# Two mixers that project convolution, keys, values and queries first and the recurrence last

## The chip, the cores and the metric

The kernel runs on one NeuronCore of a Trainium2 chip. TensorE (PE) does matmuls and transposes, VectorE (DVE) and ScalarE (ACT) the elementwise work, GpSimd (POOL) a little of it, SyncE (SP) issues nearly all loads. Each engine takes its own list of instructions strictly in order and meets the others through semaphores. The metric is the device time of one execution in microseconds.

## The reference, cut to what matters

Two conformer-like layers are followed by a state-space and mixture-of-experts block. Each of the two layers is a feed-forward part, a *mixer*, and a second feed-forward part, with a layer norm behind each. The change lies in the mixer alone:

```python
def _mixer(x, w_in, ...):
    u = x @ w_in                       # 512 tokens x 1792 columns
    u_conv, u_lru, q, k, v = jnp.split(u, [o1, o2, o3, o4], axis=-1)
    y_conv = _conv_module(u_conv, ...)  # gate, 31 taps, layernorm, silu
    y_lru = _recurrent(u_lru, ...)      # 4 taps, two gates, linear scan, * gelu
    y_attn = _swa(q, k, v, ...)         # window of 128, blocks of 128, sinks
    return jnp.concatenate([y_conv, y_lru, y_attn], axis=-1) @ w_out
```

Attention works on four blocks of 128 queries, each with 256 keys (block 0 with 128): scores, bias and mask, softmax with a sink, and the product with the values.

## The kernel before, in words

Every fp32 product of the projections is made of three fp32r matmuls (`mm3`, L114 to L116): high half by high half, high by low, low by high. So each 512 KB weight unit that is loaded into one of four `raw` buffers is split by ACT (L81, high half) and DVE (L82, low half) into `whl`. `Stream` holds the units of the whole kernel in one fixed order; a raw buffer is loaded anew as soon as it is free. In the mixers that order is: 14 units of `w_in`, 16 units of `ada_w` (the second block's modulation), 8 units of `w_out`.

The mixer's input, transposed, lies in `xTh` and `xTl`. Fourteen projections `pj(i)` read it, each 24 matmuls into one PSUM bank: 0 to 3 convolution, 4 and 5 the recurrence's input, 6 and 7 its gelu gate, 8 keys, 9 values, 10 to 13 queries. The first half of 0 to 3 is made in the stage before. What a projection leaves in its bank is taken away by a helper: `post_conv`, `post_xb` (one ACT instruction, then three DVE taps L384, giving `xc`), `post_gb` (gelu), `post_k`, `post_v`, `post_q` (`qh` by ACT L407, `ql` by DVE L408). The 31 taps of each convolution half are 62 DVE instructions (L372, L374, accumulator `acc`), put in as background work: `drain(n)` takes n of them.

`lru_gates` multiplies `xc` by gate matrices (bank `gt`, four fp32 matmuls) and takes a sigmoid; `lru_scan` does exp, tanh, square and square root on ACT, two products on POOL and a scan on DVE. `scores(b)` makes four banks `sc` on PE; DVE adds the bias and takes the maximum (L470), ACT does eight exps (L477), then DVE and ACT scale four probability tiles each (L486, L484). `pv(b)` is a generator: PE transposes the probabilities (`tp`), ACT and DVE copy them (`pT`), PE multiplies by the values (`yv`), and ACT and DVE write the result into rows 2 to 5 of `xTh` and `xTl`, over the mixer's input. `mod(n)` runs n of eight modulation steps, each four fp32 matmuls that read two raw buffers of `ada_w` (L855). `conv_ln` normalises the convolution by transposing it (`cn`, `cb`). `down` then multiplies `xTh` and `xTl` by `w_out` (`dn`, L222).

The text of the program gives priorities; a scheduler at build time sets the order on each engine from them and from its own estimate of durations. There are two mixers with the same code, stage 1 (its first 512-wide projection starts at 406.07 us) and stage 4 (1332.1 us). Each has a *first stretch* (the 512-wide projections) and a *second* (from the last projection to the first `dn`).

## Time and profile before

| | |
|---|---|
| median of 3 runs | 2941.47 us (2941.44 to 2942.12) |
| profiled execution | 2941.92 us, of which the span is 2940.1 us |
| PE busy | 2871.8 us, 98% |
| DVE busy | 1343.4 us, 46% |
| ACT busy | 1001.8 us, 34% |
| POOL busy | 188.1 us, 6% |
| HBM traffic | 158 GB/s over the span |

PE is busy nearly all the time, so a change matters by the microseconds in which PE waits, or runs at the lower clock, in the stage that is changed. The profile's line numbers are those of the kernel before; in the kernel after, everything behind the new constant stands two lines lower, and what follows the new lines of `pv` eight lower.

### The profile page before, as it was taken

What the parts mean: (1) busy time and instruction counts of PE and PEld (TensorE: products, weight loads), DVE (VectorE), ACT (ScalarE), POOL (GpSimd) and SP (SyncE); (2) the same over time, 40 slices, a digit from 0 to 9 for tenths busy, and PEclk for the clock granted to TensorE, in tenths of its full rate; (3) what the DMA queues carried; (4) which work ended last, traced back from release to release, by engine and by line L of the source; (5) the groups of instructions that cost most, each with busy time, mean ns of one, the idle gap of its engine ahead of it and who ended that gap; (6) DMA issues with size and microseconds to landing.
All of it is one profiled execution on the core that took longest, in us unless ns stands there. A gap on an engine that the chain in (4) does not pass through costs nothing.

```text
span 2940.1 us, 35337 instructions
## 1 busy us (share of the span) xinstructions
PE 2871.8 (98%) x14404; PEld 2199.5 (75%) x14404; DVE 1343.4 (46%) x2163; ACT 1001.8 (34%) x1589; POOL 188.1 (6%) x167
## 2 busy tenths in 40 slices
PE   8999998999999999999999999999999999999998
PEld 7888885888888878887588888878778886454453
DVE  4223398533335333359653234778874343222222
ACT  4222355422324122344552223567642321110011
POOL 0000001000000000001000000123330020000000
PEclk9999999999999999999999999999999999999999
DMA  6432334333323263232533323232243356899997
GB/s 196 114 99 79 94 111 153 98 104 115 93 79 98 96 205 115 78 104 79 180 118 108 98 79 105 80 108 79 87 137 130 95 206 263 341 407 427 427 427 325
DMA packets 104260, 465.93 MB, mean 158 GB/s; under 512 B 12838, under 2 KB 13494, under 8 KB 79521
## 3 DMA queue, kind: packets, MB, share of 16 engines
q1 hardware_dynamic: 95936, 435.81, 41.5%
q0 software_dynamic: 6720, 23.13, 2.7%
q10 hardware_dynamic: 1440, 4.72, 0.4%
q8 instruction: 113, 1.85, 0.2%
q14 instruction: 51, 0.41, 0.0%
HBM read 457.73 MB, written 5.88 MB: 158 GB/s over the span
## 4 chain that ended last, share of the span: by engine, by line
PE 81%; DVE 9%; DMA 6%; ACT 2%; POOL 1%; issue 1%; SPq 0%; DVEq 0%; POOLq 0%; ACTq 0%
PE dn L222 19%; PE pg L114 6%; PE pg L115 6%; PE pg L116 6%; PE pu L115 5%; PE pu L114 5%; PE pu L116 5%; DMA er<-in_eu 3%; PE ey L1673 3%; PE eu L1673 2%; PE eg L1673 2%; PE pj L115 2%; PE pj L114 2%; PE pj L116 2%; PE ga L1673 2%; DVE acc L374 2%
## 5 line engine op out<-in xcount | busy, mean ns | idle before, releaser
L82 DVE TENSOR_TENSOR whl<-raw,whl 128x1024 fp32r<-128x1024 f32 (+1 forms) x385 | 486.8, 1268 | 694.6 <-ACT whl L81 694.1
L81 ACT ACTIVATE whl<-raw 128x1024 fp32r<-128x1024 f32 (+1 forms) x385 | 405.7, 1056 | 652.3 <-PE pu L116 249.8
L222 PE MATMUL dn<-whl,hhl 128*128 128x512 f32 x2112 | 492.9, 395 | 0.0
L222 PEld LDWEIGHTS dn<-whl,hhl 128*128 128x128 f32 x2112 | 397.4, 188 | 92.4
L114 PE MATMUL pg<-xTh,whl 128*128 128x512 f32 x768 | 300.3, 391 | 0.0
L116 PE MATMUL pg<-xTh,whl 128*128 128x512 f32 x768 | 298.9, 389 | 0.0
L115 PE MATMUL pg<-xTl,whl 128*128 128x512 f32 x768 | 298.9, 389 | 0.0
L114 PE MATMUL pu<-xTh,whl 128*128 128x512 f32 x704 | 274.6, 390 | 0.0
L116 PE MATMUL pu<-xTh,whl 128*128 128x512 f32 x704 | 274.0, 389 | 0.0
L115 PE MATMUL pu<-xTl,whl 128*128 128x512 f32 x704 | 273.9, 389 | 0.0
L114 PE MATMUL pj<-xTh,whl 128*128 128x256 f32 (+1 forms) x688 | 231.4, 336 | 0.0
L115 PE MATMUL pj<-xTl,whl 128*128 128x256 f32 (+1 forms) x688 | 224.6, 326 | 0.0
L116 PE MATMUL pj<-xTh,whl 128*128 128x256 f32 (+1 forms) x688 | 224.6, 326 | 0.0
L114 PEld LDWEIGHTS pg<-xTh,whl 128*128 128x128 f32 x768 | 144.2, 188 | 36.9 <-issue 7.4
L116 PEld LDWEIGHTS pg<-xTh,whl 128*128 128x128 f32 x768 | 144.1, 188 | 30.2
L115 PEld LDWEIGHTS pg<-xTl,whl 128*128 128x128 f32 x768 | 144.3, 188 | 29.2
L292 ACT ACTIVATE sg<-pg 128x512 f32<-128x512 f32 x80 | 47.9, 598 | 320.8 <-PE pg L116 320.8
L116 PEld LDWEIGHTS pu<-xTh,whl 128*128 128x128 f32 x704 | 132.2, 188 | 27.6
L114 PEld LDWEIGHTS pu<-xTh,whl 128*128 128x128 f32 x704 | 132.1, 188 | 27.6 <-ACT x L1292 0.2
L115 PEld LDWEIGHTS pu<-xTl,whl 128*128 128x128 f32 x704 | 132.1, 188 | 27.4 <-issue 0.2
L295 DVE SCALAR_TENSOR_TENSOR h<-sg,pu 128x512 f32<-128x512 f32 x74 | 50.9, 688 | 198.9 <-PE pu L116 198.9
L115 PEld LDWEIGHTS pj<-xTl,whl 128*128 128x128 f32 x688 | 131.4, 191 | 10.9 <-issue 0.5
(485 smaller groups left out, 3996.4 us busy)
## 6 DMA issues: line engine op xcount, KB each, us to landing
raw<-in_wgu SPq DMA_DIRECT2D x176, 512.0 KB, 3.5
er<-in_eu SPq DMA_DIRECT2D x64, 1024.0 KB, 19.0
er<-in_eg SPq DMA_DIRECT2D x64, 1024.0 KB, 18.0
er<-in_ed SPq DMA_DIRECT2D x56, 1024.0 KB, 19.2
raw<-in_wd SPq DMA_DIRECT2D x88, 512.0 KB, 3.5
raw<-in_win SPq DMA_DIRECT2D x76, 512.0 KB, 3.5
raw<-in_ada_w SPq DMA_DIRECT2D x48, 512.0 KB, 4.5
raw<-in_wout SPq DMA_DIRECT2D x16, 512.0 KB, 5.0
```

The lines of the kernel that those rows point to most:

```text
L81: k.nc.scalar.activation(hi, r, AF.Copy)
L82: k.nc.vector.tensor_tensor(out=lo, in0=r, in1=hi.bitcast(F32), op=OP.subtract)
L114: mm(out, l[0], r[0], start=start, stop=False)
L115: mm(out, l[0], r[1], start=False, stop=False)
L116: mm(out, l[1], r[0], start=False, stop=stop)
L222: nc.tensor.matmul(banks[t, dh], l[:, s], r[:, dh * 512:(dh + 1) * 512], start=(u == 0 and n_l == 0), stop=(u == last and n_l == 2))
L292: nc.scalar.activation(sg, pg, AF.Silu)
L295: return nc.vector.scalar_tensor_tensor(h, sg, 0.5, pu, op0=OP.mult, op1=OP.mult)
L374: nc.vector.scalar_tensor_tensor(acc[:, j:], y[:, :T - j], wj, acc[:, j:], op0=OP.mult, op1=OP.add)
L1673: return tc.keep_in_program_order(nc.tensor.matmul(*args, **kw))
```

## The change

The order of the mixer's work is rewritten. After the convolution's projections come keys, values and the four queries; then the scores of block 0, projection 4, the scores of block 1, projection 5, the four gate products, block 0's product with the values, projection 6, the scores of block 2, projection 7, block 1's product with the values between the two scans, and the scores of block 3. The weight units are loaded in the same order (`MIXER`). Since projections 6 and 7 still read `xTh`, block 0's result can't be written there yet: ACT copies it from PSUM into a spare tile `yv` first, and the two writes follow later. The modulation steps stand behind projection 7, behind block 1 and behind the scores of block 3; those that are left follow in `mod(16)` as before.

```diff
@@ -27,6 +27,8 @@
 AHEAD = 2
 RAWS = 4
 SPLITS = 7
+
+MIXER = (0, 1, 2, 3, 8, 9, 10, 11, 12, 13, 4, 5, 6, 7)
 MODS = {1: {13: 1}, 3: {f: 1 for f in range(6, 14)}, 4: {13: 1}}
 PER = 1
 ROWS = {1: (0,), 3: (1,), 4: (2,)}
@@ -353,7 +355,7 @@
             w.ensure(u + 4)
             self.proj(u, bank[i], cols)
             w.done(u)
-            self.mod(MODS[st].get(i, 0))
+            self.mod(MODS[st].get(MIXER.index(i), 0))
 
         conv = []
 
@@ -508,6 +510,12 @@
                     nc.tensor.matmul(y[g * 64:g * 64 + 64], vn[0][:, vb * 128 + g * 64:vb * 128 + g * 64 + 64], pt[g],
                                      start=(kb == kbs[0]), stop=(kb == 1))
                 yield
+            if b == 0:
+
+                t = self.unit(name="yv")
+                nc.scalar.activation(t, y, AF.Copy)
+                y = t
+                yield
             bs = slice(b * 128, b * 128 + 128)
             yv = y.rearrange("p (r q) -> p r q", r=4)
             nc.scalar.activation(self.xTh[:, 2:6, bs], yv, AF.Copy)
@@ -553,54 +561,48 @@
                 post_conv(i // 2)
                 self.bg += [lambda c=i // 2, j=j: tap(c, j) for j in range(TAPS)]
             self.drain((0, 0, 4, 4)[i])
-        for c in range(2):
-            pj(4 + c)
-            post_xb(c)
-            self.drain(3)
-        for c in range(2):
-            pj(6 + c)
-            self.drain(7)
         self.load_band()
-        for c in range(2):
-            lru_gates(c)
-        for c in range(2):
-            post_gb(c)
         pj(8)
         post_k()
-        lru_scan(0)
-        self.drain(6)
+        self.drain(5)
         pj(9)
         post_v()
-        lru_scan(1)
-        self.drain(6)
+        self.drain(5)
         for r in range(4):
             pj(10 + r)
             post_q(r)
-            self.drain(6)
+            self.drain(5)
             if r == 0:
                 v_nat()
+        run = lambda *gs: [0 for g in gs for _ in g]
+        scores(0)
+        pj(4)
+        post_xb(0)
+        self.drain(3)
+        scores(1)
+        pj(5)
+        post_xb(1)
+        for c in range(2):
+            lru_gates(c)
+        p0 = pv(0)
+        for _ in range(3):
+            next(p0)
+        pj(6)
+        self.drain(3)
+        scores(2)
+        pj(7)
+        run(p0)
+        for c in range(2):
+            post_gb(c)
+        lru_scan(0)
+        run(pv(1))
+        self.mod(PER)
+        lru_scan(1)
+        self.drain(5)
+        scores(3)
+        self.mod(PER)
         for c in range(2):
             self.split_to(c, lru[c])
-        per = PER
-        run = lambda *gs: [0 for g in gs for _ in g]
-        scores(0)
-        self.drain(5)
-        self.mod(per)
-        scores(1)
-        self.drain(5)
-        self.mod(per)
-        p0 = pv(0)
-        next(p0)
-        self.mod(per)
-        run(p0)
-        scores(2)
-        self.drain(5)
-        self.mod(per)
-        p1 = pv(1)
-        next(p1)
-        self.mod(per)
-        run(p1)
-        scores(3)
         self.drain(1000)
         cl = conv_ln()
         run(zip(range(3), cl))
@@ -1956,9 +1958,11 @@
                     else:
                         steps, back = a["wgu"][l, j // 2], a["wd"][l, j // 2]
                     todo = self.mods(st)
-                    self.u_in[st] = []
+                    self.u_in[st] = [None] * 14 if j == 1 else []
                     for i in range(14 if j == 1 else NF):
-                        for m in range(steps[i].shape[0]):
+                        if j == 1:
+                            self.u_in[st][MIXER[i]] = w.add(steps[MIXER[i]][0])
+                        for m in range(0 if j == 1 else steps[i].shape[0]):
                             self.u_in[st].append(w.add(steps[i][m]))
                         n = MODS.get(st, {}).get(i, 0)
                         self.add_mod(todo[:n])
```

On PE, before, the first rows show the gate products (`gt`) among the projections, and the end of the last projection with a modulation step and the first scores (`sc`) behind it.

```order
L116 MATMUL pj<-xTh,whl 128x512
L423 MATMUL gt<-xc,lruw 128x512 x4
L114 MATMUL pj<-xTh,whl 128x512
...
L116 MATMUL pj<-xTh,whl 128x512
L855 MATMUL mod<-raw,cs 32x512 x4
L463 MATMUL sc<-kh,qh 128x128 x2
```

On PE, after, the first piece stands between projections 5 and 6, the second behind projection 7.

```order
L118 MATMUL pj<-xTh,whl 128x512
L425 MATMUL gt<-xc,lruw 128x512 x4
L500 MATMUL tp<-ident,S 128x128 x8
L510 MATMUL yv<-pT,vn 64x512 x2
L116 MATMUL pj<-xTh,whl 128x512
...
L118 MATMUL pj<-xTh,whl 128x512
L857 MATMUL mod<-raw,cs 32x512 x4
L500 MATMUL tp<-ident,S 128x128 x8
L857 MATMUL mod<-raw,cs 32x512 x17
L510 MATMUL yv<-pT,vn 64x512 x2
```

The gates, block 0's transposes and its product now stand in front of projection 6, and 21 of the 32 modulation matmuls stand around block 1's transposes, behind all projections.

On DVE, before, the taps of the recurrence (`xc`) alternate with the convolution's (`acc`) while PE does projections.

```order
L374 SCALAR_TENSOR_TENSOR acc<-yin,pc,acc 128x505
L384 SCALAR_TENSOR_TENSOR xc<-pj,pc,xc 128x511
L374 SCALAR_TENSOR_TENSOR acc<-yin,pc,acc 128x504
L384 SCALAR_TENSOR_TENSOR xc<-pj,pc,xc 128x510
L374 SCALAR_TENSOR_TENSOR acc<-yin,pc,acc 128x503
```

On DVE, after, the first `xc` stands among the work of the softmax of blocks 0 and 1 (`ISA` is the bias and maximum of L470, `sm` the softmax's small columns).

```order
L376 SCALAR_TENSOR_TENSOR acc<-yin,pc,acc 128x492
L481 TENSOR_TENSOR sm<-sm 128x8
L472 ISA S,sm<-sc,bias,sinks 128x256
L472 ISA sm 128x1
L482 RECIPROCAL sm<-sm 128x8
L386 SCALAR_TENSOR_TENSOR xc<-pj,pc,xc 128x511
L488 TENSOR_SCALAR S<-S,sm 128x128 x4
L386 SCALAR_TENSOR_TENSOR xc<-pj,pc,xc 128x510
L472 ISA S,sm<-sc,bias,sinks 128x256
L472 ISA sm 128x1
L386 SCALAR_TENSOR_TENSOR xc<-pj,pc,xc 128x509
```

The recurrence's taps moved behind all of block 0's and part of block 1's bias and maximum, and behind convolution taps that stood elsewhere before.

On ACT, after, the piece from block 0's `pT` to the exp of the first scan reads as follows.

```order
L505 ACTIVATE pT<-tp 128x512
L516 ACTIVATE yv<-yv 128x512
L417 ACT_TABLE_LOAD
L417 ACTIVATE gl<-pj 128x512
L479 ACT_TABLE_LOAD
L479 ACTIVATE S,sm<-S,sm 128x256 x8
L480 ACTIVATE sm<-sm 128x8
L521 ACTIVATE xTh<-yv 128x4x128
L486 ACTIVATE S<-S,sm 128x256 x4
L417 ACT_TABLE_LOAD
L417 ACTIVATE gl<-pj 128x512
L435 ACT_TABLE_LOAD
```

Before, one table load served both gelus and stood ahead of all exps of the softmax; now gelu and exp alternate, and the copy to the spare tile stands in between.

## Rows read from the trace of the kernel before

**Rows 1.** Windows: us, busy us (x) of PE, PEld, DVE, ACT, POOL; clock; DMA; GB/s.

```profile
406.07:464.54 58.47, 58.47 (x255) 46.79 (x253) 54.92 (x70) 24.78 (x32) 9.33 (x6) 1.00 0.20 66
464.54:508.08 43.54, 33.66 (x224) 16.53 (x223) 32.56 (x121) 28.27 (x88) 1.87 (x3) 0.86 0.67 231
...
1390.60:1435.07 44.47, 34.01 (x227) 16.58 (x226) 32.77 (x122) 29.49 (x93) 2.57 (x4) 0.88 0.68 228
```

**Rows 2.** Waits of PE, 390 to 560 us: us in total, times, longest.

```profile
PE sc L463 <- DVE ql L408: 3.4, 1, 3.4
PE yv L508 <- ACT pT L503: 3.0, 1, 3.0
...
PE tp L498 <- DVE S L486: 1.6, 1, 1.6
```

**Rows 3.** Waits of PE, 1320 to 1500 us.

```profile
PE yv L508 <- ACT pT L503: 2.5, 2, 2.2
...
PE dn L222 <- DVE ab L864: 1.9, 1, 1.9
```

**Rows 4.** Timeline of PE: start, duration in us, then the instruction; idle before.

```profile
427.86 3.59 PE L423 MATMUL gt<-xc,lruw 128*128 128x512 f32 x8
...
486.53 0.39 PE L463 MATMUL sc<-kh,qh 64*128 64x256 f32 x2
...
488.16 1.09 PE L498 MATMUL tp<-ident,S 128*128 128x128 f32 x8
489.18 3.26 PE L855 MATMUL mod<-raw,cs 128*32 128x512 f32 x14
492.37 1.07 PE L508 MATMUL yv<-pT,vn 128*64 128x512 f32 x2
...
503.71 1.97 PE L508 MATMUL yv<-pT,vn 128*64 128x512 f32 x2 [3.00 <-ACT pT L503]
...
508.08 1.20 PE L222 MATMUL dn<-whl,xTh 128*128 128x512 f32 x2
```

**Rows 5.** Timeline of DVE, same columns.

```profile
412.55 0.75 DVE L384 SCALAR_TENSOR_TENSOR xc<-pj,pc,xc 128x511 f32<-128x511 f32 x1
413.22 0.73 DVE L374 SCALAR_TENSOR_TENSOR acc<-yin,pc,acc 128x504 f32<-128x504 f32 x1
413.87 0.74 DVE L384 SCALAR_TENSOR_TENSOR xc<-pj,pc,xc 128x510 f32<-128x510 f32 x1
...
459.46 4.57 DVE L374 SCALAR_TENSOR_TENSOR acc<-yin,pc,acc 128x497 f32<-128x497 f32 x6
463.94 0.68 DVE L408 SCALAR_TENSOR_TENSOR ql<-pj,qh 128x512 fp32r<-128x512 f32 x1
...
474.71 0.35 DVE L470 CUSTOM_DVE_ANT_0 S<-sc,bias,sinks 128x128 f32<-128x128 f32 x1
...
474.98 0.34 DVE L470 CUSTOM_DVE_ANT_0 S<-sc,bias,sinks 128x128 f32<-128x128 f32 x1
...
477.28 0.48 DVE L470 CUSTOM_DVE_ANT_0 S<-sc,bias,sinks 128x256 f32<-128x256 f32 x1
...
477.68 0.48 DVE L470 CUSTOM_DVE_ANT_0 S<-sc,bias,sinks 128x256 f32<-128x256 f32 x1
```

**Rows 6.** Timeline of ACT, same columns.

```profile
432.20 1.28 ACT L415 ACT_TABLE_LOAD   x1
433.49 1.09 ACT L415 ACTIVATE gl<-pj 128x512 f32<-128x512 f32 x2
...
485.52 1.71 ACT L484 ACTIVATE S<-S,sm 128x256 f32<-128x256 f32 x4
...
492.19 0.51 ACT L477 ACTIVATE S<-S,sm 128x256 f32<-128x256 f32 x1 [2.67 <-DVE sm L473]
...
496.13 0.19 ACT L478 ACTIVATE sm<-sm 128x8 f32<-128x8 f32 x1
```

**Rows 7.** Line 63 (loads to raw buffers), 463 to 500 us.

```profile
DMA to landing us min/median/max: 3.6/4.7/8.1
```

## The prediction

> **What bounds the kernel now.** I read the shares of busy time first (PE 98%), then windows over the first mixer's two stretches, then PE's waits there, then the timelines of PE, DVE and ACT, and last the time that a load takes to land. The windows show where time can be won. In the first stretch, 58.47 us, PE is busy throughout at full clock, with DVE busy 54.92 of it. In the second, 43.54 us, PE is busy 33.66 and the granted clock is 0.86; the second mixer's is alike, 44.47 and 34.01 [rows 1]. PE waits there for `ql`, for `pT` and for scaled probabilities [rows 2], in the second mixer for `pT` and, at the first `dn`, 1.9 us for DVE's `ab` [rows 3]. After its 3.0 us wait a `yv` product takes 1.97 us where one at full clock takes 1.07 [rows 4]: PE is at its lower level of 1.2 GHz until about the first `dn`.
>
> What PE would need there at full clock: 32 modulation matmuls at 0.456 (14 records, two to a matmul, in 3.19 us), 14.6; 40 transposes at 0.125, 5.0; 7 `yv` at 0.5, 3.5; 48 score pairs, 5.7 (a block of 256 keys takes 1.5, from 486.53 to 488.16); 8 `cn`, 1.1 [rows 4]. That is 29.9, so 13.6 of 43.54 us are waiting and low clock. Both mixers lose some 27 us: more than that can't be won.
>
> **The change, step by step (first mixer).** Up to 406.07 nothing moves. A projection takes 5.46: the first stretch less 3.5 for the gates [rows 4] and 0.4 for a transpose, over 10 [rows 1].
>
> *Queries.* Six projections and the transpose end at 439.2. The last `ql` follows six convolution taps on DVE; at 0.65 each where two accumulators alternate (the `acc` between two `xc`) [rows 5] it ends at 441.3, and PE waits 1.1 at the end of block 0's scores, against 3.4 [rows 2].
>
> *The recurrence's gates.* Projection 4 ends at 447.0, block 1's scores at 448.5, projection 5 at 453.9. Then PE wants `xc`. DVE's list from that `ql` to the last tap of the second `xc`: 8 bias-and-maximum at 0.27 and 8 at 0.40, 5.4; 6 `xc` taps at 0.65, 3.9; 15 convolution taps, of which 8 follow their own accumulator at 0.75 (six in 4.48 us) and 7 alternate at 0.65, 10.6; scaling and small columns 1.5 [rows 5]. Sum 21.4: the second `xc` is there at 462.7, the first at 455.5. PE waits 1.6, does two gates (1.7), waits 5.5 and does two more.
>
> *Block 0.* ACT can start block 1's exps only at 458.8, behind DVE; eight take 3.94, the table for the sigmoid 1.28, a gate 0.6, four scalings 1.65, three gates 1.8, `pT` 0.6 [rows 6]: 468.7, and DVE's `pT` about 469.5. PE's transposes were done at 465.5, so it waits 4.0. It resumes at 470.5 with projection 6, after 12.2 us of waiting since 439. None of the modulation steps, which fill PE's waits before, stands here.
>
> *The clock.* PE did little from 454 to 470, so projection 6 will begin at 1.2 GHz, as the `yv` at 503.71 does. No row shows a projection after such a wait; bounds are 0 and 5.5, the whole of it at half speed. The nearest row, that `yv`, lost 0.9; I take 1.2. Projection 7 then ends at 484.2. PE has 23.7 us left to the first `dn` (29.9 less four of the scores, transposes and products done): 507.9 without any wait, where before has 508.08 [rows 4]. So the gain is gone by here, and each later wait is a loss.
>
> *Modulation.* With four raw buffers two of eight steps are loaded; 17 matmuls then stand in one piece and reach into the sixth step. A pair of buffers is freed, loaded and used again in 0.9 plus a landing. Landings there took 3.6 to 8.1 us, median 4.7 [rows 7]; I take 4.5. Steps 1 and 2 are done at 489, steps 3 to 5 at 492, 494.7, 497.5, the sixth's first matmul at 498.7; block 1's product, block 3's scores, `cn`, the last steps, block 2's transposes follow, with a wait for step 8's buffers. The first `dn` is due about 513.4, 5.5 us of waits later than without any.
>
> *The first units of `w_out`.* Their buffers come free only with step 7, at about 507; before, they were asked for at 491. The first split ends at 513, just in time. Behind it on ACT stand the exp table (1.28) and block 3's eight exps (3.94) and only then the second split (1.05): 519.3 [rows 6]. PE has 9 `dn` and a product to do, 2.6 us, and waits about 3.3.
>
> *Costed at nothing:* the copy to the spare tile (0.6 on ACT, in a stretch where ACT waits for projection 6), and the recurrence's last POOL and DVE work, which ends before the first `dn`. Block 3's probabilities are ready near 521, `dn`'s list reaches them near 526; if that cover fell away it would cost up to 2.
>
> *Sum:* 513.4 − 508.08 + 3.3 = 8.6, say 9 in the first mixer; in the second 7, since the 1.9 at `dn` is hidden there. 16 us on the profiled execution's 2941.9 (span 2940.1 and 1.8 around it; 0.5 above the median of the runs): **2958**.
>
> A page speaks against the change more strongly: the Trainium skill, ScalarE: Activation LUTs, "What ACT_TABLE_LOAD costs", counts a drain of some 1.4 us on top of each load's 1.28. The trace shows the load at 432.20 and the gelu that needs it at 433.49 [rows 6], so 1.28 is all of it here. By the page the five loads between block 0's copy and block 1's `pT` would delay that `pT` by 6.9 more, past PE's 498.7, and the later ones on the way to the second split by 4.2: some 2966.
>
> **Rivals.**
>
> *Break even.* The waits behind projection 7 vanish, because loads land at 3.6 and the second split is taken ahead of the exps' end. For it: the first-stretch sum gives 507.9. Against: ACT's own chain to block 1's `pT` (exps of block 2 from 483, scaling, two gelus apart, exp, tanh, square, square root, three tables) ends near 496.5, with 13 us of PE's list behind it: 509.5. Time: −1 to +2 a mixer, 2940 to 2946.
>
> *Faster.* Projections 4 to 7 cover the softmax. It needs `xc` by 455.6, a DVE list of 14 us instead of 21.4, say because taps of different accumulators are in truth spread elsewhere. Then 12.2 of waiting shrinks to about 3, and the first `dn` comes 9 us earlier: 2941.9 − 18 = 2924. For it: before, PE's waits are all for this softmax, and 22 us of projections now lie beside it. Against: DVE was already busy 54.92 of 58.47 [rows 1], and what is added there delays `xc`. The Trainium skill, Perfetto Trace Analysis, "Optimization Strategy", says that interleaving regimes with different busiest engines may help; the trace agrees that DVE is the busier beside PE in the first stretch too, which leaves little to interleave.
>
> *Much slower.* Loads land at 8.1, the slowest row, since twelve `ada_w` units now come in a bunch. Three generations of buffers at 3.4 to 3.6 more each cost 10 a mixer: 2978. It decides from a landing of about 6 on.
>
> That the change doesn't do what it says is excluded by the order on the engines.
>
> **How the numbers follow.** Forecast 0.58, break even 0.15, faster 0.15, much slower 0.12. The unknowns move the forecast: landing 3.6 takes 2.7 from each mixer, the clock takes 1.2 or adds up to 4.3; its own range is 2948 to 2968. For 8 in 10 I leave out most of the faster case and half of the slowest: 2938 to 2972. 0.2% (5.9 us) is about what a measurement of this kernel can tell from no change. Faster by more: 0.15. Within: the break-even case less a little, 0.14. Slower: 0.71.
>
> **What would show it.** In the changed kernel's waits: `gt` waiting for DVE's `xc` some 7 us in two pieces; `yv` for `pT` 4 us; `mod` and its weight loads for `ada_w` several us; `dn` for ACT's `whl` 3 us; projection 6 begun at a lower granted clock; the first `dn` some 107 us behind the first 512-wide projection, before 102.0. The forecast is wrong if `xc` comes within 2 us of the end of projection 5, or if the modulation steps run without a wait for loads.

## The result: 38 us slower, where 16 were forecast

The changed kernel takes 2979.8 us (median of 4 runs, 2976.9 to 2983.0), the kernel before 2941.8 beside it (2941.4 to 2942.5): a ratio of 1.0129, 95% interval 1.0116 to 1.0141. The direction was forecast, the size was not: 2979.8 lies above the range of 2938 to 2972. The profiled execution spans 2978.8 us against 2940.1.

### Where the 38 us lie

Read the end of each mixer at the first `tb`, the transposes behind `w_out`. It came at 552.76 in the kernel before and comes at 569.17 now, of which 0.9 was there before the first mixer; for the second mixer it was 1478.33 and is 1516.79. So the first mixer lost 15.5 us, the second 22.0 (38.5 less 16.4), and the rest of the kernel next to nothing. This is one execution; in that of `e8` below, which differs from the changed kernel by little, the two mixers take 18.6 and 20.2 us more than before, so the two are less unlike than 15.5 and 22.0 say. Windows of the changed kernel over the first mixer, cut where [rows 1] are cut and once more at the end:

```profile
406.96:465.40 58.44, 51.89 (x253) 40.70 (x252) 57.70 (x119) 21.78 (x55) 0.00 (x0) 0.98 0.20 66
465.40:516.88 51.48, 44.76 (x226) 20.89 (x224) 24.55 (x73) 30.61 (x56) 9.80 (x9) 0.89 0.49 156
516.88:569.17 52.29, 47.36 (x198) 32.93 (x197) 24.46 (x46) 25.69 (x48) 4.77 (x6) 0.97 0.41 133
```

The last stretch of the kernel before, which [rows 1] do not have:

```profile
508.08:552.76 44.68, 44.68 (x196) 33.15 (x195) 24.20 (x46) 20.68 (x34) 4.76 (x6) 0.98 0.37 111
```

PE's idle time is the window less its busy time: 18.2 us over the three windows, 9.9 before (58.47 + 43.54 + 44.68 less 136.81). Nearly the same number of matmuls, 677 for 675, was busy 7.2 us longer. Waits grew by 8.3 and busy time by 7.2 in this mixer; together they are the 15.5.

Not all of the 7.2 is the clock. These are the stretches of the changed kernel's first mixer in which the granted clock was 0.50, so 1.2 GHz:

```profile
463.50:466.91 3.41, 3.41 (x4) 1.26 (x5) 3.41 (x10) 3.38 (x7) 0.00 (x0) 0.50 0.01 2
490.80:497.63 6.83, 5.80 (x18) 0.75 (x16) 1.89 (x3) 4.60 (x7) 1.27 (x1) 0.50 0.97 337
511.28:514.70 3.42, 3.31 (x12) 0.90 (x8) 3.14 (x16) 0.00 (x0) 1.94 (x4) 0.50 1.03 349
521.52:524.93 3.41, 3.41 (x6) 1.05 (x6) 2.90 (x8) 3.41 (x7) 1.17 (x2) 0.50 0.44 175
```

And these are those of the kernel before:

```profile
468.81:475.63 6.82, 5.28 (x38) 3.28 (x42) 6.75 (x23) 0.00 (x0) 0.00 (x0) 0.50 0.45 145
502.94:509.77 6.83, 6.06 (x18) 4.17 (x19) 4.56 (x12) 6.69 (x21) 1.91 (x4) 0.50 0.63 232
```

PE was busy for 15.9 us at the lower level, 11.3 before. If work at that level takes twice its time, the lower clock cost 8.0 us against 5.7, so 2.3 of the 7.2 (an estimate from these rows). The other 4.9 are spread over several products, and nothing here takes them apart. A part of them is that PE's work comes in shorter pieces: a modulation step whose two buffers have landed takes 1.07 us (x8, at 464.54 below), and half a step that runs alone, since the second buffer is not there yet, takes nearly as long:

```profile
489.15 1.05 PE L857 MATMUL mod<-raw,cs 128*32 128x512 f32 x4 [1.88 <-DMA raw<-in_ada_w]
```

PE's waits in the changed kernel, first mixer (390 to 580 us), against [rows 2]:

```profile
PE gt L425 <- ACT S L479: 5.2, 1, 5.2
PE mod L857 <- DMA raw<-in_ada_w: 5.2, 5, 1.9
PE dn L224 <- DVE ab L866: 3.4, 1, 3.4
PE yv L510 <- DVE pT L503: 1.5, 1, 1.5
PE yv L510 <- ACT pT L505: 1.4, 1, 1.4
PE gt L425 <- issue: 0.8, 1, 0.8
PE sc L465 <- DVE ql L410: 0.6, 1, 0.6
```

And in the second (1330 to 1520 us), against [rows 3]:

```profile
PE mod L857 <- DMA raw<-in_ada_w: 7.5, 6, 2.7
PE dn L224 <- DVE ab L866: 6.8, 1, 6.8
PE gt L425 <- ACT S L479: 5.2, 1, 5.2
```

Here the name behind an arrow needs care. "gt <- ACT S" names the exponentials, because they ended last before the matmul ran; what the gate reads is `xc`, and VectorE's third tap of the second `xc` ended at 463.29, just before the gate's matmul.

```profile
462.54 0.75 DVE L386 SCALAR_TENSOR_TENSOR xc<-pj,pc,xc 128x509 f32<-128x509 f32 x1
463.44 3.65 PE L425 MATMUL gt<-xc,lruw 128*128 128x512 f32 x4 [5.19 <-ACT S L479]
```

The chain of loads can be followed through three engines. On PE, the first modulation step of the mixer:

```profile
484.18 1.07 PE L857 MATMUL mod<-raw,cs 128*32 128x512 f32 x8
```

On SyncE's queue (start, and the time until the last of the group is issued), the loads behind that step:

```profile
410.39 97.01 SPq L65 DMA_DIRECT2D raw<-in_ada_w  x16
508.39 24.71 SPq L65 DMA_DIRECT2D raw<-in_wout  x8
```

On ScalarE, the first split of `w_out`, and what stands behind it:

```profile
514.85 1.06 ACT L83 ACTIVATE whl<-raw 128x1024 fp32r<-128x1024 f32 x1 [5.19 <-DMA raw<-in_wout]
515.92 1.28 ACT L479 ACT_TABLE_LOAD   x1
517.22 0.51 ACT L479 ACTIVATE S<-S,sm 128x256 f32<-128x256 f32 x1
```

The four raw buffers are full by 424 us with two steps' weights, and until the first step frees one the DMAs stand almost still, as the window up to it shows (share 0.03):

```profile
424.00:484.18 60.18, 52.23 (x260) 38.50 (x258) 49.38 (x122) 27.03 (x72) 2.90 (x2) 0.97 0.03 10
```

From the first step to `w_out`'s first split it takes 30.7 us. In the kernel before it took 32.2, but began 19.6 us earlier (0.9 of it from before the mixer). Its step on PE:

```profile
464.54 1.07 PE L855 MATMUL mod<-raw,cs 128*32 128x512 f32 x8
```

And its first split on ScalarE:

```profile
496.71 1.04 ACT L81 ACTIVATE whl<-raw 128x1024 fp32r<-128x1024 f32 x1
```

There the split stood 11.4 us ahead of the first `dn` at 508.08 [rows 4]; now the first `dn` follows it by 2.0.

The second thing that moved is the recurrence. PE had written block 3's scores by 505.0, but on VectorE their reductions stand behind the second scan:

```profile
508.89 1.23 DVE L444 TENSOR_TENSOR_SCAN hs<-av,gate 128x512 f32<-128x512 f32 x1 [0.27 <-POOL gate L442]
510.03 0.46 DVE L472 CUSTOM_DVE_ANT_0 S<-sc,bias,sinks 128x256 f32<-128x256 f32 x1
```

So block 3's exponentials came to stand behind `w_out`'s first split on ScalarE (515.92 and 517.22 above), and the second split behind them, at 521.26. On GpSimd the load of modulation's bias into `ab` stands behind the recurrence's last product:

```profile
510.19 1.27 POOL L445 TENSOR_TENSOR hs<-hs,gl 128x512 f32<-128x512 f32 x1 [1.34 <-DVE hs L444]
511.40 0.74 POOL L865 DMA_DIRECT2D ab<-in_ada_b  x1
```

In the kernel before it was issued 30 us earlier, at 481.55. VectorE can add it at 520.57 only, 9.2 us after its issue:

```profile
520.57 0.69 DVE L866 TENSOR_TENSOR ab<-ab,mod 128x512 f32<-128x512 f32 x1 [3.41 <-DMA ab<-in_ada_b]
```

And on PE `dn`, which takes over modulation's PSUM bank, waits for that:

```profile
516.88 0.84 PE L224 MATMUL dn<-whl,xTh 128*128 128x512 f32 x2
...
521.31 1.07 PE L224 MATMUL dn<-whl,xTh 128*128 128x512 f32 x2 [3.37 <-DVE ab L866]
```

In the second mixer, where the wait for the bias is twice as long (6.8), the recurrence is not what holds the load. Between its last product and the bias stands a load into `cs`, the tile that modulation's matmuls read, and that load waits for the last of them, which ended at 1458.48:

```profile
1455.72 1.27 POOL L445 TENSOR_TENSOR hs<-hs,gl 128x512 f32<-128x512 f32 x1 [1.34 <-DVE hs L444]
1458.79 0.59 POOL L1528 DMA_DIRECT2D cs<-in_iota  x1 [1.81 <-PE mod L857]
1459.38 0.73 POOL L865 DMA_DIRECT2D ab<-in_ada_b  x1
1468.76 0.69 DVE L866 TENSOR_TENSOR ab<-ab,mod 128x512 f32<-128x512 f32 x1 [6.86 <-DMA ab<-in_ada_b]
```

The kernel before has the same order there (1423.32 and 1423.90) and waits 1.9 us [rows 3]. So this wait hangs on modulation's last matmul, not on the recurrence's last product.

### The profile page after: what moved, and what is told of

The parts are those of the page before. It is cut to its first block, busy times and chain, and to the rows that moved or that the text cites. A ratio compares the mean times of both kernels' runs of the same rounds, so it can differ in the third digit from the quotient of the medians.

```text
span 2978.8 us, 35351 instructions
## 1 busy us (share of the span) xinstructions
PE 2890.5 (97%) x14404; PEld 2200.7 (74%) x14404; DVE 1332.2 (45%) x2163; ACT 1011.0 (34%) x1597; POOL 187.5 (6%) x167
## 4 chain that ended last, share of the span: by engine, by line
PE 78%; DVE 9%; DMA 8%; ACT 2%; POOL 1%; issue 1%; SPq 0%; DVEq 0%; ACTq 0%; POOLq 0%
PE dn L224 18%; PE pg L116 6%; PE pg L118 6%; PE pg L117 6%; PE pu L118 5%; PE pu L117 5%; PE pu L116 5%; DMA er<-in_eu 3%; PE ey L1675 3%; PE eu L1675 2%; PE eg L1675 2%; PE pj L116 2%; PE pj L117 2%; PE pj L118 2%; DVE acc L376 2%; PE ga L1675 2%
## 5 line engine op out<-in xcount | busy, mean ns | idle before, releaser
L116 PEld LDWEIGHTS pj<-xTh,whl 128*128 128x128 f32 x688 | 131.5, 191 | 12.3 <-issue 1.6
```

The costliest lines, as they stand in the source:

```text
L116: mm(out, l[0], r[0], start=start, stop=False)
```

## The experiments

Times below are medians, and their distance from the kernel before as measured beside them on the same chip; the changed kernel stands 38.0 over it. Waits are PE's, over the whole kernel (two mixers), from each kernel's profile. Diffs are cut and stand against the changed kernel, where nothing else is said. The first theory was that three waits (gates, modulation's loads, the bias) each cost their own length.

**The bias load, early** (`e1_bias_early`).

```diff
...
         if k == 0:
             st["ps"] = self.ps("mod")
+            if r != 1:
+                self.ab_load(r)
...
-            ab = self.unit(name="ab")
...
-            nc.gpsimd.dma_start(ab, src)
...
+            ab = st["ab"]
```

> The changed kernel with one DMA moved: the load of modulation's bias into `ab` is issued at modulation's first step of a mixer, ahead of the recurrence's products on GpSimd, and no longer at its last step behind them. Theory (the bias load is a cost of its own: VectorE's `ab` add, which frees modulation's PSUM bank and has `modc`, the transposes' copies and the splits queued behind it, came 3.4 us late in the first mixer and 6.8 us late in the second): both `dn` waits on `ab` go, w_out's second split shows instead (1 to 2 us a mixer), and about 9 us come back: 2971. Rival (that wait only covers another, w_out's second split behind the eight exponentials of block 3 on ScalarE): at most 2 us come back, 2978 or more, and the same time is shown as a wait for `whl`.

Measured: 2973.4, 30.0 over (before 2943.3), so 8.0 came back, as the theory had it. But the list of waits follows the rival: `ab` is gone from it, and `dn` waits 6.6 us for `whl` instead, where it waited 1.0 (4.4 on ScalarE, 2.2 on VectorE); the profile's first mixer even ends later, at 571.08. Part of that wait was a cover.

**Taps later** (`e2_taps_later`).

```diff
             post_q(r)
-            self.drain(5)
+            self.drain(3)
...
         post_xb(0)
-        self.drain(3)
         scores(1)
...
         pj(6)
-        self.drain(3)
+        self.drain(8)
...
         run(p0)
+        self.drain(6)
```

> The changed kernel with 11 of the convolution's taps in each mixer moved from the stretch of the last queries and projection 4 to behind projections 6 and 7 (drains of 3 instead of 5 after each query projection, none after projection 4, 8 and 6 behind 6 and 7). Theory (VectorE's list, busy 57.7 of 58.4 us, is what the gates wait for: 6.0 us a mixer): the gates wait under 2 us, and 6 to 10 us come back where the later stretch hides the taps: 2971. Rival (the later stretch is set by loads and by the recurrence, not by when projection 7 ends, so what the gates save is waited for at modulation's loads): 2978 to 2981, with over 8 us of gates' waits gone and as much more waiting for ada_w. Second rival: the taps now delay the layer norm and the kernel is slower, 2985.

Measured: 2970.9, 27.5 over. The time is the theory's, the reason is not: the gates wait 11.1 us against 12.0, in two pieces of 5.5 now read as "gt <- DVE xc". With 11 taps less, the second `xc` simply stood behind block 1's reductions, exponentials and scaling: ScalarE began it at 457.28, after the last of eight exponentials. What came back is behind them: the first modulation step began at 480.62, 3.6 us earlier (0.9 of it from before the mixer), and `w_out`'s second split at 514.03 instead of 521.26.

**Modulation early** (`e3_mods_early`).

```diff
-MODS = {1: {13: 1}, 3: {f: 1 for f in range(6, 14)}, 4: {13: 1}}
+MODS = {1: {i: 1 for i in range(10, 14)}, 3: {f: 1 for f in range(6, 14)}, 4: {i: 1 for i in range(10, 14)}}
```

> The changed kernel with one modulation step behind each of projections 4, 5 and 6 as well as behind 7 (two steps stay with blocks 1 and 3, two at the end), so ada_w comes through SyncE's queue between the last projections' weights, where the DMA share was 0.2. Theory (modulation's last seven steps wait for loads because four raw buffers turn over once a landing, and w_out's loads stand behind them): waits of modulation on loads fall from 12.7 to under 4 us, the step behind projection 5 fills 2 us of the gates' wait, w_out is split 8 us earlier, and 14 to 18 us come back: 2963. Rival (modulation's raw buffers keep the weights of projections 6 and 7 out, so these wait for loads and splits): 2978 or more, with a wait for `whl` at `pj`.

Measured: 2968.9, 25.5 over; 12.5 came back. `w_out`'s first split is at 496.28, 18.6 us earlier and not 8, and no `dn` waits. But new waits stand in their place: `tp` for VectorE's `sm` 13.0, `yv` for `pT` 9.3. With the loads out of the way, the lists of ScalarE and VectorE end as late.

**The order of the projections alone** (`e4_order_alone`). All scores, attention and modulation stand behind the last projection, as in the kernel before, and the gates and scans of the recurrence stand there too. The diff is against the kernel before.

```diff
-        for c in range(2):
-            pj(4 + c)
-            post_xb(c)
-            self.drain(3)
-        for c in range(2):
-            pj(6 + c)
-            self.drain(7)
         self.load_band()
...
         for r in range(4):
             pj(10 + r)
...
+        for c in range(2):
+            pj(4 + c)
+            post_xb(c)
+            self.drain(3)
+        for c in range(2):
+            pj(6 + c)
+            self.drain(6)
+        for c in range(2):
+            lru_gates(c)
+        for c in range(2):
+            post_gb(c)
+        lru_scan(0)
+        lru_scan(1)
...
         scores(0)
```

> One part of the change alone: the projections in the new order (convolution, keys, values, queries, then recurrence and its gate), but all scores, attention and modulation behind the last projection as in the kernel before, the gates and the recurrence there too, and no spare tile. Theory (the loss comes from what stands between the projections and from the recurrence that ends late): the gates have xc by then, first `dn` waits for the bias load, which stands behind the recurrence's products: 2948 to 2956, part of the loss only. Rival (the order of the projections costs nothing, the loss is all in the interleaving): 2940 to 2944. Second rival (the late recurrence is the whole loss): 2970 or more.

Measured: 2961.7, 18.3 over (ratio 1.0062, 1.0050 to 1.0075), more than the theory had. Modulation begins at 460.94, earlier than in the kernel before, and the bias makes nobody wait. The place is VectorE's and ScalarE's queues. PE has written the scores of block 0 by 467.0, but on VectorE their reduction stands behind the second scan:

```profile
481.90 1.22 DVE L444 TENSOR_TENSOR_SCAN hs<-av,gate 128x512 f32<-128x512 f32 x1 [2.10 <-POOL gate L442]
483.04 0.33 DVE L472 CUSTOM_DVE_ANT_0 S<-sc,bias,sinks 128x128 f32<-128x128 f32 x1
```

and on ScalarE block 0's exponentials behind the recurrence's functions and their tables, from 466.38 on:

```profile
480.48 1.28 ACT L479 ACT_TABLE_LOAD   x1
487.68 0.40 ACT L479 ACTIVATE S<-S,sm 128x128 f32<-128x128 f32 x1 [5.92 <-DVE sm L475]
```

The softmax starts 16 us behind its scores, at 483.04 (at 472.36 in the kernel before), because the recurrence no longer runs under the projections of keys, values and queries, where the kernel before has it.

**The three together** (`e5_all_three`). The diffs of the first three, in one kernel.

> The changed kernel with the three edits of before together: bias load early, taps later, modulation's steps behind projections 4 to 7. Alone they stood 30, 27.5 and 25.5 us over the kernel before where the changed kernel stands 38 over it. Theory (three separate costs, one behind another on the path): the gains add, 8 + 10.5 + 12.5 = 31 of 38, so about 7 over the kernel before, 2949. Rival (each edit only uncovers what stands behind it, ScalarE's and VectorE's lists above all, and the late recurrence sets the end): the three together gain little over the best alone, 20 us over before or more, 2962.

Measured: 2985.2, 42.3 over: slower than any of the three, and no faster than the changed kernel (38.8 to 48.0 by its interval, the changed kernel 34.1 to 41.5). No gate waits, no `dn` waits; `yv` waits 35.1 us (12.8, 11.3 and 11.0). This ended the theory of three separate costs: each edit alone moved a wait to another place, with some gain; together they seem to have moved everything in front of the same lists, which no run takes apart.

**`xc` first** (`e7_xc_first`).

```diff
-        scores(1)
         pj(5)
         post_xb(1)
+        scores(1)
```

> The changed kernel with projection 5 and the recurrence input made from it put ahead of block 1's scores, and nothing else. Theory (with 11 taps less in the list the gates still waited 5.5 us a mixer, since the second recurrence input stands in the queues of ScalarE and VectorE behind block 1's eight exponentials, reductions and scalings): the gates wait under 3 us a mixer and not 6, 6 to 8 us come back, 2972. Rival (the backlog of taps on VectorE, as forecast): the gates wait 4 us a mixer or more, under 3 us come back.

Measured: 2985.4, 42.5 over, 4.5 more than the changed kernel, but the intervals overlap (38.0 to 46.2 and 34.1 to 41.5): nothing came back, and whether it is slower is not shown. The gates wait 6.1 instead of 12.0 us, about what the theory had, and nothing comes of it:

```profile
PE yv L510 <- ACT pT L505: 19.2, 2, 9.6
```

The row comes from PE's waits, whole kernel; in the changed kernel `yv` waited 4.6 us for `pT`. It seems that two lists decide when block 0's attention and the gates are both done, and that what PE meets first only names the wait.

**The recurrence early again** (`e6_recurrence_early`). `lru_out` is the product with the gelu, which was the scan's last line.

```diff
-MIXER = (0, 1, 2, 3, 8, 9, 10, 11, 12, 13, 4, 5, 6, 7)
+MIXER = (0, 1, 2, 3, 4, 5, 8, 9, 10, 11, 12, 13, 6, 7)
...
+        for c in range(2):
+            pj(4 + c)
+            post_xb(c)
+            self.drain(3)
         pj(8)
...
+            lru_gates(c)
...
+        lru_scan(0)
...
+                lru_scan(1)
...
         scores(0)
-        pj(4)
-        post_xb(0)
+        pj(6)
...
-        scores(2)
         pj(7)
         run(p0)
         for c in range(2):
             post_gb(c)
-        lru_scan(0)
+            lru_out(c)
+        scores(2)
+        self.drain(5)
+        self.mod(PER)
...
```

Two more things move with it: block 2's scores now stand behind projection 7, and a modulation step behind them.

> The recurrence's inputs (projections 4 and 5), its gates and its scan go back ahead of the queries, under the projections of keys, values and queries; only the gate projections 6 and 7 stay between the scores, and the product with their gelu comes behind them. Spare tile, block 0 early, and modulation behind the second block stay. Theory (the loss is the recurrence behind the queries: its ScalarE chain of 18 us with its table loads and the gates' waits have no projections over them any more; the order alone showed +18 of it): no gates' wait over 1 us, no wait on `ab`, and projections 6 and 7 fill what the kernel before waited for at `sc`, `tp` and `yv`: 2924 to 2938, faster than the kernel before. Rival (the loss is in the projections between the scores: PE in-order, low clock, loads of modulation later): 2950 or more.

Measured: 2956.9, 14.0 over: 24 of the 38 are gone, but the kernel before is not beaten. No gate and no `ab` wait is left, and block 3's exponentials stand ahead of `w_out`'s splits again, three of which now run in one piece:

```profile
500.72 0.51 ACT L481 ACTIVATE S<-S,sm 128x256 f32<-128x256 f32 x1 [0.60 <-DVE sm L477]
512.42 2.94 ACT L83 ACTIVATE whl<-raw 128x1024 fp32r<-128x1024 f32 x3
```

`tp` waits 9.0 us for VectorE's scaling of block 0, and the first `dn` of each mixer waits 3.85 for `w_out`'s first split: modulation begins at 479.42, nearly as late as in the changed kernel, and the split comes 33.0 us behind it.

**No spare tile** (`e8_no_spare`).

```diff
-            if b == 0:
-                t = self.unit(name="yv")
-                nc.scalar.activation(t, y, AF.Copy)
-                y = t
-                yield
...
-        for _ in range(3):
+        for _ in range(2):
```

> The changed kernel without the spare tile: block 0's attention output stays in its PSUM bank until projection 7 has read the rows of the stage's input that it overwrites. Theory (the copy cost nothing): 2977 to 2982. Rival (a PSUM bank held for two projections makes `pj`, `sc` or `tp` wait for one): 2985 or more.

Measured: 2978.6, 35.7 over. The copy against a PSUM bank held longer makes no difference that can be told.

**Both early** (`e9_early_both`): the recurrence as in `e6`, and modulation's first steps behind the last query projection, 6 and 7, the later ones each a block earlier.

```diff
-MODS = {1: {13: 1}, 3: {f: 1 for f in range(6, 14)}, 4: {13: 1}}
+MODS = {1: {i: 1 for i in range(11, 14)}, 3: {f: 1 for f in range(6, 14)}, 4: {i: 1 for i in range(11, 14)}}
```

> The kernel with the recurrence under keys, values and queries again, and with modulation's first steps early as well: one behind the last query projection, one behind projection 6, one behind 7, the others behind blocks 0, 1 and 2. Theory (two things set the end side by side: the chain of loads, 29 to 33 us in every kernel of this order from modulation's first step to w_out's first split, since four raw buffers turn over once a landing; and the lists of ScalarE and VectorE, with the recurrence in them where it stands behind the queries. Either edit alone left the other): w_out's first split is some 20 us earlier, first `dn` waits for no split, the modulation steps fill the 4.5 us that `tp` waited for block 0: 11 to 20 us less than with the recurrence early alone, 2937 to 2946. Rival (the softmax lists with the taps in them set the end in this order too): 2952 or more, the waits move to `tp` and `yv`.

Measured: 2951.2, 9.8 over, between theory and rival. `w_out`'s first split is at 507.47, only 5 us earlier than in `e6`, since PE reaches the middle steps late; `tp` still waits 9.6, `yv` 7.4, and one `dn` 6.0 for `ab`, in the second mixer, where the bias load stands behind the one into `cs`. No run moves that load alone.

**Half of modulation's loads** (`e10_half_loads`).

```diff
-            for j in range(2):
+            for j in range(2 if r == 1 else 1):
                 self.w.add(self.a["ada_w"][0, k * 128:(k + 1) * 128, (2 * r + j) * D:(2 * r + j + 1) * D], split=False)
...
-        r0, r1 = w.get(u), w.get(u + 1)
+        r0 = w.get(u)
+        r1 = w.get(u + 1) if r == 1 else r0
...
```

> The changed kernel with half of modulation's loads in the mixers left out: each step reads its first weight tile twice, so ada_w's second half of each row pair is not used; the matmuls, their number and all else stay. Theory (the chain of loads from modulation's first step to w_out is one of the two bounds of the mixer's end): from that step to w_out's first split 31 us become 20 or less, the 12.7 us of modulation's waits go, 12 to 22 us come back, 2958 to 2968. Rival (the lists of ScalarE and VectorE, with the recurrence in them, end as late without the loads): the waits go from modulation to `yv`, `cn` and `dn` on VectorE and ScalarE, under 6 us come back, 2974 or more.

This kernel leaves half of modulation's weights out. Measured: 2967.5, 26.1 over; 11.9 came back, the theory's lower edge. From the first step (482.64) to `w_out`'s first split (494.70) it is 12.1 us, and as in `e3` the lists are what is left:

```profile
PE tp L500 <- DVE sm L472: 13.0, 2, 6.5
PE yv L510 <- ACT pT L505: 10.8, 4, 5.6
PE gt L425 <- ACT S L479: 10.4, 2, 5.2
```

**The converse in the kernel before** (`e11_before_mods_late`; the diff is against it).

```diff
-MODS = {1: {13: 1}, 3: {f: 1 for f in range(6, 14)}, 4: {13: 1}}
+MODS = {1: {}, 3: {f: 1 for f in range(6, 14)}, 4: {}}
...
         scores(0)
         self.drain(5)
-        self.mod(per)
         scores(1)
         self.drain(5)
-        self.mod(per)
```

> The converse in the kernel before: its order of projections, recurrence and scores as they are, and modulation's first three steps of a mixer (behind the last query projection, blocks 0 and 1) only behind the first transposes of block 0, some 19 us later, as late as in the changed kernel. Theory (the late first modulation step alone carries a large part of the loss, by the chain of loads to w_out): w_out's first split 31 us behind that step, some 18 us later than before, first `dn` 8 to 10 us later, and as much again behind it where splits come one by one: 2957 to 2972. Rival (modulation is filler, and the recurrence behind the queries is the loss): 2941 to 2947.

Measured: 2962.4, 21.0 over (ratio 1.0070, 1.0057 to 1.0083). PE's and ScalarE's rows repeat the changed kernel's chain, 31.7 us from step to split, with nothing else of the change in the kernel:

```profile
481.56 3.26 PE L853 MATMUL mod<-raw,cs 128*32 128x512 f32 x16
...
514.35 0.73 PE L222 MATMUL dn<-whl,xTh 128*128 128x512 f32 x2 [1.21 <-ACT whl L81]
```

```profile
513.24 1.06 ACT L81 ACTIVATE whl<-raw 128x1024 fp32r<-128x1024 f32 x1 [4.42 <-DMA raw<-in_wout]
```

First `dn` comes 6.3 us later than in [rows 4]. The other part is that the steps no longer fill PE's waits: `tp` waits 13.8 us, `sc` 8.7, where the kernel before has 4.2 and 6.7. So the 21.0 are not the price of the loads alone: PE's waits for loads and for splits grew by 6.3 (`mod` 5.8 for 1.8, `dn` 4.2 for the 1.9 it waited for the bias), those at `tp` and `sc` by 11.6, and the first `dn` found its split 1.2 us late only.

**Three more, on the 10 us that `e9` still loses.** Taps held back until a block's probabilities are scaled (`e12_taps_out`, on `e9`; `e14_before_taps_out`, on the kernel before), and a second modulation step behind the last query projection of the kernel before (`e13_before_two_mods`).

The taps in `e12`, against `e9`, where `scaled` is the last scaling of a block on VectorE (`e14` holds back all that are left behind block 0's scores in the same way):

```diff
         pj(6)
-        self.drain(3)
+        with self.tc.issue_after(self.scaled.ins):
+            self.drain(3)
...
         run(p0)
+        with self.tc.issue_after(self.scaled.ins):
+            self.drain(1000)
```

The step in `e13`, against the kernel before:

```diff
-MODS = {1: {13: 1}, 3: {f: 1 for f in range(6, 14)}, 4: {13: 1}}
+MODS = {1: {13: 2}, 3: {f: 1 for f in range(6, 14)}, 4: {13: 2}}
```

> The kernel with recurrence and modulation early (10 us over the kernel before), and the last 23 taps of the convolution held back on VectorE until block 0's, then block 1's probabilities are scaled. Theory (the taps inside block 0's softmax hold the rest: VectorE ran 3 of them ahead of its first reduction and 7 between its maximum and its scaling, and `tp` waited 4.8 us a mixer): `tp` waits under 2 us a mixer, 5 to 9 us come back, 2942 to 2947. Rival (the rest hangs on loads: four buffers and a PE that stands at later instructions, 53 us from the first modulation step to w_out's first split): under 2 us come back, the wait moves to modulation's loads or `yv`.

> The kernel before with two modulation steps and not one behind the last query projection, and one fewer at the end; nothing else. Theory (in the kernel before w_out's first split stands 11 us ahead of its first use, so the chain of loads does not set the end there, and the step only moves PE's work into the 3.4 us that the scores wait for `ql`): 2937 to 2942, the wait at `sc` 2 us shorter a mixer, given back in part at `tp`. Rival (one step earlier in the chain of loads is worth as much as 19 us later cost, about 1 us per us): 2934 or less.

> The kernel before with the taps that stood behind the last query projection held back on VectorE until block 0's probabilities are scaled; nothing else. Theory (taps in the softmax of block 0 cost there too: `sc` waits 3.4 us for `ql`, which this leaves, and `tp` and the scaling wait behind 4 taps between the reductions): 2935 to 2940, `tp` waits 1 to 2 us less a mixer. Rival (VectorE has idle time behind, and the layer norm of the convolution now comes later and holds first `dn` or `cb`): 2941 to 2946.

Measured: `e12` 2948.4, 7.0 over, so 2.8 came back of the 5 to 9 expected, and even that is not clear of noise (4.1 to 9.4 over by its interval, `e9` 5.3 to 12.6); `tp` waits 6.5 instead of 9.6 (4.2, 1.7 and 0.6), `yv` 11.1. `e14` 2939.1 against 2941.3 (ratio 0.9987 to 1.0005): the wait at `tp` fell from 4.2 to 0.4, no difference in time that can be told. `e13` 2938.5 against 2941.3, ratio 0.9989 (0.9980 to 0.9998): the wait at `sc` fell from 6.7 to 5.0, `yv` rose from 5.5 to 6.0. It is the one version here that beats both kernels, by 0.1%, and its interval only just leaves out no change. The theory's 2 us at `sc` a mixer were 0.9.

## Why the prediction was wrong

*Queries.* Right: PE waited 0.6 for `ql` (forecast 1.1; [rows 2]: 3.4).

*The recurrence's gates.* The size was right, 6.0 us in two pieces (forecast 7.1), and VectorE's list was as long as counted (463.29, forecast 462.7). The reason was only half of it: `e2` shows that without 11 of its taps the second `xc` is still late, behind block 1's softmax.

*Block 0.* `pT` 1.4 us late, not 4.0; projection 7 ended where forecast, at 484.18 (forecast 484.2). That it fits so well is partly luck: the waits up to there were some 4 us shorter than forecast, and the later start (0.9), two gates at the lower clock (3.65 for 1.96) and the work between took that back.

*The clock.* Priced at 1.2 (bounds 0 and 5.5), at the start of projection 6. That place was wrong: the clock was 0.50 from 463.50 to 466.91, in the last two gates, and projections 6 and 7 ran at 1.00:

```profile
471.20:484.18 12.98, 12.98 (x73) 10.33 (x72) 3.57 (x18) 6.47 (x15) 0.00 (x0) 1.00 0.01 1
```

Over the whole mixer the lower clock cost 2.3 us more than before (the estimate above), inside the bounds. What the sum did not see is that the clock fell three times behind projection 7.

*What PE needs.* The 14.6 us for modulation were taken from a piece of 14 records [rows 4] in which the buffers land one after another. A step with both buffers there takes 1.07, so eight take 8.6; measured were 12.4 before and 16.4 now, the lower clock included. The 29.9, the 507.9 and the most that can be won rest on that price.

*Modulation, and `w_out`'s first units.* The mechanism was right: halving the loads gave 11.9 back (`e10`), and the chain's rows come again in the converse (`e11`). Modulation waited 5.2 us (forecast 5.5); `w_out`'s first split ended at 515.9 (forecast 513), the second at 522.3 (forecast 519.3), first `dn` came at 516.88 (forecast 513.4). The forecast's wait at `dn` for ScalarE, 3.3 a mixer, lay under the wait for the bias; with the bias early (`e1`) it is 6.6 in two mixers. For both mixers the forecast had 2 × 8.8 = 17.6 us in this chain. `e11`'s 21.0 are no test of that size, since they hold unfilled waits too.

*The step that failed* is the one "costed at nothing": the recurrence's last work, "which ends before the first `dn`". It did end before (the product at 511.46), but that is not what it costs. Moved behind the queries, the recurrence stands in in-order queues in front of what others wait for: the softmax on VectorE and ScalarE, in the first mixer the bias load on GpSimd. The order alone cost 18.3 us (`e4`), and putting the recurrence back into the changed kernel gave 24 (`e6`, which moves block 2's scores and a modulation step with it, so it is not the recurrence alone).

How the 38.0 divide is not shown. The recurrence taken back is worth 24, the loads halved or early 11.9 to 12.5 (`e10`, `e3`). `e11` and `e4`, each alone against the kernel before, make 21.0 + 18.3 = 39.3, close to the 38.0 (34.1 to 41.5), but that is no proof: their waits (`tp` and `sc` in `e11`, `sc` and `yv` in `e4`) are not those of the changed kernel (`gt`, `mod`, `dn`), and `e5` shows that parts do not add here.

*The sum* failed in its last terms: it closed at the second split and took "the 1.9 at `dn`" [rows 3] as hidden in the second mixer. It came as 3.4 in the first and 6.8 in the second, where the bias load waits for the end of modulation; the forecast itself had that end later than before. Counted from the first 512-wide projection, first `dn` came 7.9 us later than before in the first mixer and 12.2 in the second, and what stands behind it took 7.6 and 9.8 longer; the forecast had 5.3 and 3.3 for the first and 7 in all for the second, which it did not work out for itself.

*Tables.* The Trainium skill, ScalarE: Activation LUTs, "What ACT_TABLE_LOAD costs", counts a drain of some 1.4 us beside the load at every switch of the table set. The changed kernel's rows do not show one: the split ends at 515.91, the table load at 515.92 takes 1.28, and the exponential begins at 517.22, 0.02 after it. The loads cost by their place in the queue, not by a drain.

*The rivals.* "Much slower" gave 2978, a time near the measured one, from loads landing at 8.1 us; the median landing was 5.2 for `ada_w` and 7.1 for `w_out`, and halving the loads gave back 11.9 of 38. It was the right neighbourhood for a part of the reason. "Faster" needed `xc` by 455.6; its last tap ended at 463.29. Its 2924 also left out the 5.5 and 3.3 us that the forecast has behind projection 7; with them the same sum gives about 2940.

Still open: what holds the last 7 us of `e12`, where recurrence, modulation and taps are all out of the way. Its waits (`yv` 11.1, modulation's loads 6.8) suggest that two projections between the scores do not fill more than the modulation steps filled before, but no run takes that apart.

## What to carry to other kernels

Before moving a stage, list for every in-order queue that it issues into what would then stand behind it, and who waits for that; a stage that "ends in time" can still hold a queue. A step that frees buffers sets when the next weights can be loaded: read the chain from that step to its last consumer as one duration (here 31 us), and ask by how much the step moves. When taking away a wait brings a new one of the same length elsewhere, the bound is a list on another engine, and the wait's name is only the place where PE met it.

## What the runs showed that was not expected

The load chain keeps its length over very different kernels: 29.3 to 33.8 us from the first modulation step to `w_out`'s first split, over both mixers of both kernels and of `e1`, `e2`, `e6`, `e7`, `e8` and `e11`, while its start in the first mixer moved by 22 us (464.54 to 486.77). Where ScalarE comes late to the split it is longer (35.8 in `e4`). And removing a wait could bring nothing (`e7`), though the instruction waited for came earlier; three edits that gave 8.0, 10.5 and 12.5 us alone gave nothing together (`e5`).
